# One-hots of the gates with two tokens innermost instead of four, and the steps of pair choice and gates dealt out over u's blocks

## The chip, the cores and the metric

The kernel runs on one NeuronCore of one Trainium2 chip. The metric is the device time of one execution in microseconds. The kernel before took 2054.61 us, the median of three runs (2054.53 to 3795.32). TensorE is called PE below, VectorE DVE, ScalarE ACT, GpSimd POOL and the queue that issues the DMAs SP.

## What is computed

Two transformer layers over 256 tokens of width 1024: an attention mixer with a projection in and out (in layer 0 a sparse one, in layer 1 one with a forget gate), and behind each mixer the expert network `peer_ffn`, which takes most of the time:

```python
def peer_ffn(x, w_q, sub_keys, u, v):
    q = (x @ w_q).reshape(B, S, PEER_HEADS, 2, hq)
    s_half = jnp.einsum('bshpc,hpkc->bshpk', q, sub_keys).astype(jnp.float32)
    top_s, top_i = lax.top_k(s_half, PEER_TOPK)                  # 16 of 128, twice per head
    cand_s = top_s[..., 0, :, None] + top_s[..., 1, None, :]
    cand_i = top_i[..., 0, :, None] * PEER_N_KEYS + top_i[..., 1, None, :]
    best_s, best_pos = lax.top_k(cand_s.reshape(B, S, PEER_HEADS, n_cand), PEER_TOPK)
    experts = jnp.take_along_axis(cand_i.reshape(B, S, PEER_HEADS, n_cand), best_pos, axis=-1)
    gate = jax.nn.softmax(best_s, axis=-1)
    ...
        h = jax.nn.gelu(jnp.einsum('ted,td->te', u[ec], xc))
        return jnp.einsum('te,ted->td', gc.astype(h.dtype) * h, v[ec])
```

Each token chooses 8 x 16 experts out of 16384 = 128 x 128. An expert's number is a pair of keys.

## The kernel before

The expert network is computed densely. In each layer `peer` walks over the 128 blocks of `u` (128 experts each). For one block, `load_split` (L679) fetches 512 KB, ACT rounds it to the matmul's short fp32 format (`hi`, L116) and DVE takes the rest (`lo`, L117); three buffers of each rotate. `feat_block` (L695) then makes 24 matmuls of 256 columns: `hi` by the tokens' high part (L699), `hi` by their low part (L702) and `lo` by their high part (L703). `values` (L921) applies gelu and multiplies by the gates of that block: where a token's gate is there already, DVE does it (L930); where it isn't, the gelu is stored (L926) and multiplied later. Behind u comes the same walk over the 128 blocks of `v` (L965 to L967), which gives the output. A stage ahead of u projects the queries (16 blocks of `wq`) and scores them against the keys on DVE (L733 to L737).

Between u's blocks the program issues other work in small steps, written as Python generators that yield after each step:

- `best_pairs` (L802 to L877), pair choice: for each half of the tokens (`tt`), DVE adds the candidates (L817), takes the best 16 per head (L824 to L828), turns positions into indices by masks and sums (L834, L837, L841, L847, L848, L852, L855, L859) and normalises the gates (L862 to L867). Then PE transposes the indices and gates (L872 to L874) and they are copied to `hkT`, with a token per column.
- `gate_steps` (L890 to L919), gates: for 8 tokens at a time DVE compares `hkT`'s rows with `iota` and gets one-hots `o2` and `oh` of fp16 (L898, L899), multiplies `oh` by the gate's low part into `ol` and by its high part in place (L901, L902); PE makes, per token, two matmuls with the one-hot `o2` as weights and `oh` or `ol` as the moving operand, 128 columns each (L908, L909): 16 matmuls, called a cluster below, of which there are 32 per layer. DVE multiplies the result into blocks that have their values already (L915); ACT stores it for the others (L917).

In the one-hots' tiles the order is group, key, token: with four tokens innermost, the 128 elements that one matmul reads lie four fp16 elements, 8 bytes, apart.

How many steps are issued behind each block is set at the end of `peer`: `now` counts a price per step (0.8 for any step of pair choice, 1.3 for any of the gates) and steps are taken while it is under 1.5 per block. Pair choice has 24 steps per half, 48 in all; the gates have 96. The order in which engines execute is not the issue order alone: a scheduler lists the instructions per engine by what it holds to be ready, and each engine then works strictly down its list. Instructions in `pin` keep program order.

At the very start (`nsa`, L302 to L350) PE gets matmuls whose result nobody reads: `keep_warm(8)`, 8 of 512 columns on bf16 zeros, then `keep_warm_r`, 30 on fp32 zeros (10 each of 256, 192 and 128 columns, L318), then the transposes of the first piece of x (`norm.piece`, L150), `keep_warm(3)`, and the first projection (L327, L328, L333).

Of the kernel before, what the change touches and what calls it, by code (L numbers as in the profile page):

```python
# [17 lines left out]
P = 128  # L18
# [21 lines left out]
def body(ctx, tc, A, out):  # L40
# [13 lines left out]
    maskb = const.tile([P, P], BF16, name="maskb")  # L54
    iota = const.tile([P, 2, P, 4], F16, name="iota")
    dram = ctx.enter_context(tc.tile_pool(name="dram", bufs=1, space=bass.MemoryType.DRAM))
# [51 lines left out]
    def late_consts():  # L108
        V.tensor_copy(identb, ident)
        GP.iota(iota, pattern=[[0, 2], [1, P], [0, 4]], base=0, channel_multiplier=0, allow_small_or_imprecise_dtypes=True)  # L110
        mtmp = t2k(P)
        SP.dma_start(mtmp, A["cmask"])
        V.tensor_copy(maskb, mtmp)
# [146 lines left out]
    def nsa():  # L260
# [50 lines left out]

        V.memset(HL[:, 12288:12288 + S].bitcast(F32), 0.0)
        wz = HL[:, 12288:12288 + S]

        def keep_warm_r(n, w):
            pt = pst("h")
            for _ in range(n):
                pin(PE.matmul(pt[:, :w], wz[:, :P], wz[:, :w], start=True, stop=True))  # L318

        o = [pst("m", bufs=4) for _ in range(2)]  # L320
# [15 lines left out]
        keep_warm(8)  # L336
        for w in (S, 192, P):
            keep_warm_r(10, w)
        norm.piece(0, 0, True)
# [366 lines left out]
    def peer(li, norm):  # L706
# [95 lines left out]
        def best_pairs():  # L802

            for tt in range(2):
# [4 lines left out]
                for a in range(9):  # L809
                    n = CAND_N[a] if a < 8 else 8  # L810
                    if a < 8:
                        i0 = top[:, tt, :, 1, 0:n]
                        i1 = top[:, tt, :, 0, a:a + 1].broadcast_to((P, 8, n))
                    else:
                        i0 = top[:, tt, :, 0, 8:16]
                        i1 = top[:, tt, :, 1, 0:1].broadcast_to((P, 8, n))
                    V.tensor_tensor(cand[:, tt, :, o_:o_ + n], i0, i1, ALU.add)  # L817
                    o_ += n
                    if a in (2, 8):
                        yield  # L820
                for hh in range(8):
                    c1 = cand[:, tt, hh]
                    c2 = cand2[:, hh % 2]
                    V.max(best[:, tt, hh, 0:8], c1)  # L824
                    V.max_index(pos[:, tt, hh, 0:8], best[:, tt, hh, 0:8], c1)
                    V.match_replace(c2, best[:, tt, hh, 0:8], c1, FMIN)
                    V.max(best[:, tt, hh, 8:16], c2)
                    V.max_index(pos[:, tt, hh, 8:16], best[:, tt, hh, 8:16], c2)  # L828
                    yield
                V.tensor_tensor(gf[:, tt], best[:, tt], best[:, tt, :, 0:1].broadcast_to((P, 8, 16)), ALU.subtract)  # L830

                V.tensor_copy(posh[:, tt], pos[:, tt])
                for hh in range(8):
                    V.tensor_tensor(msk[0][:, hh], posh[:, tt, hh].unsqueeze(1).broadcast_to((P, 16, 16)), st3, ALU.is_ge)  # L834
                    if hh % 4 == 3:
                        yield
                V.tensor_tensor(msk[0], msk[0], dl[:, tt].unsqueeze(3).broadcast_to((P, 8, 16, 16)), ALU.mult)  # L837
                yield
                for q in range(2):
                    hs = slice(4 * q, 4 * q + 4)  # L840
                    V.tensor_reduce(i12[:, tt, 0, hs], msk[0][:, hs].rearrange("p h j k -> p h k j"), AX.X, ALU.add)  # L841
                    yield

                V.tensor_scalar(bh[:, tt], posh[:, tt], -42.0, 0.0, ALU.add, ALU.max)
                V.tensor_tensor(bh[:, tt], posh[:, tt], bh[:, tt], ALU.subtract)
                for i, (st, ln) in enumerate(((16, 16), (24, 8), (29, 5), (33, 4), (36, 3), (38, 2), (40, 2), (42, 2))):
                    V.tensor_scalar(th[:, tt], posh[:, tt], float(st), float(ln), ALU.is_ge, ALU.mult)  # L847
                    V.tensor_tensor(bh[:, tt], bh[:, tt], th[:, tt], ALU.subtract)  # L848
                    if i % 4 == 3:
                        yield  # L850
                for hh in range(8):
                    V.tensor_tensor(msk[1][:, hh], bh[:, tt, hh].unsqueeze(1).broadcast_to((P, 16, 16)), jt3, ALU.is_equal)  # L852
                    if hh % 4 == 3:
                        yield
                V.tensor_tensor(msk[1], msk[1], idxh[:, tt, :, 1, :].unsqueeze(3).broadcast_to((P, 8, 16, 16)), ALU.mult)  # L855
                yield
                for q in range(2):
                    hs = slice(4 * q, 4 * q + 4)
                    V.tensor_reduce(i12[:, tt, 1, hs], msk[1][:, hs].rearrange("p h j k -> p h k j"), AX.X, ALU.add)  # L859
                    yield  # L860
                g3 = gf[:, tt]
# [5 lines left out]
                V.tensor_tensor(g3, g3, gs.unsqueeze(2).broadcast_to((P, 8, 16)), ALU.mult)  # L867
                yield

# [6 lines left out]
                V.tensor_tensor(hkT[:, 3, ts], pt[:, 2 * P:3 * P], hkT[:, 2, ts], ALU.subtract)  # L876
                yield  # L877

# [11 lines left out]
        def gate_steps():  # L890


            for t0 in range(0, S, 8):
                ohb, ol = t4k(2, 2, P, 4, dt=F16), t2k(2, P, 4, dt=F16)
                o2, oh = ohb[:, 0], ohb[:, 1]
                row = lambda i: (hkT[:, i, t0:t0 + 8].rearrange("p (q t) -> p q t", q=2)
                                 .unsqueeze(2).broadcast_to((P, 2, P, 4)))
                V.tensor_tensor(o2, iota, row(1), ALU.is_equal)  # L898
                V.tensor_tensor(oh, iota, row(0), ALU.is_equal)  # L899
                yield  # L900
# [10 lines left out]
                yield  # L911
                for q in range(2):
# [5 lines left out]
                    done[1] += 4  # L918
                yield  # L919

# [11 lines left out]

        aux = [(0.8, x) for x in (best_pairs,)] + [(1.3, gate_steps)]
        now, (cost, steps) = 0.0, (aux[0][0], aux[0][1]())
        aux.pop(0)
        for b in range(NB):
            values(b, feat_block(load_split(uT[b])))
            while steps is not None and now < 1.5 * (b + 1):
                if next(steps, 0) == 0:
                    cost, steps = (aux[0][0], aux[0][1]()) if aux else (0, None)  # L940
                    aux = aux[1:]
                now += cost
        for _ in steps or ():
            pass

# [156 lines left out]
```

## Time and profile before

| | us |
|---|---|
| median of three runs | 2054.61 |
| the profiled execution | 2047.41 |
| its span from first to last instruction | 2045.5 |
| u's walk, layer 0 (matmul starts to the last block's end) | 253.5 to 700.6 |
| u's walk, layer 1 | 1241.8 to 1689.0 |

The profile is of one execution. An engine's busy time counts matmuls that overlap in the pipeline with their whole length each, so a busy PE is judged here by how far apart its matmuls start and by how many there are in a stretch, not by its busy share. [...]

### The profile page before, as it was taken

Reading aid. Unit: us, or ns where it says so; the run is one execution under the profiler, and the core shown is the slowest. Engines: PE = TensorE matmul, PEld = TensorE weight load, DVE = VectorE, ACT = ScalarE, POOL = GpSimd, SP = SyncE. Lnnn points to the kernel's source line nnn. Section 1 sums busy time; section 2 is a strip of 40 time slices with the busy share of each in tenths; the row PEclk is TensorE's granted clock in tenths of the full one; section 3 lists DMA queues with packets and bytes.
Section 4 is the critical chain, followed back from the end, with each engine's and each line's share of the span. In section 5 each row is a group of like instructions: output and inputs, shape, how many; then the busy total and the mean of one; then the engine's idle time right before and its main releaser. Section 6 shows DMA issues by size and latency. Waiting matters only on the chain.

```text
span 2045.5 us, 34104 instructions
## 1 busy us (share of the span) xinstructions
PE 1995.8 (98%) x13121; PEld 1782.2 (87%) x13121; DVE 1422.5 (70%) x2973; ACT 1001.7 (49%) x1912; POOL 154.5 (8%) x98
## 2 busy tenths in 40 slices
PE   9999989999999999999999999999999999999998
PEld 6747989999999988888879799999999998888886
DVE  7576999677777555555576789976777755555555
ACT  5454644544444444444464654544444454444444
POOL 3010700000000000000050251000000000000001
PEclk9989999999999999999999999999999999999999
DMA  7701545444445676666664234544444456666664
GB/s 283 251 27 62 155 136 165 149 149 137 148 141 156 208 234 195 216 192 193 193 227 166 68 120 148 167 145 144 145 146 141 149 177 194 196 214 200 193 195 144
DMA packets 90193, 340.91 MB, mean 167 GB/s; under 512 B 9872, under 2 KB 12336, under 8 KB 84656
## 3 DMA queue, kind: packets, MB, share of 16 engines
q1 hardware_dynamic: 89744, 338.22, 52.6%
q8 instruction: 103, 1.69, 0.3%
q14 instruction: 58, 0.48, 0.1%
q10 hardware_dynamic: 288, 0.52, 0.1%
HBM read 334.48 MB, written 4.19 MB: 166 GB/s over the span
## 4 chain that ended last, share of the span: by engine, by line
PE 76%; DVE 16%; issue 4%; ACT 3%; DMA 1%; POOL 0%; SPq 0%; ACTq 0%; DVEq 0%
PE m L966 11%; PE m L965 11%; PE m L967 11%; PE h L703 8%; PE h L702 7%; PE h L699 7%; DVE lo L117 4%; PE m L908 3%; PE m L909 3%; ACT hi L116 3%; PE m L200 2%; PE m L201 2%; PE m L202 2%; DVE vhl L902 1%; DVE vraw L901 1%
## 5 line engine op out<-in xcount | busy, mean ns | idle before, releaser
L117 DVE TENSOR_TENSOR lo<-raw,hi 128x1024 fp32r<-128x1024 f32 x512 | 628.2, 1227 | 432.0 <-ACT hi L116 429.0
L116 ACT CAST hi<-raw 128x1024 fp32r<-128x1024 f32 (+1 forms) x576 | 577.4, 1005 | 671.6 <-PE m L967 293.4
L703 PE MATMUL h<-xh,lo 128*128 128x256 f32 x2048 | 583.9, 285 | 8.8 <-DVE lo L117 8.7
L702 PE MATMUL h<-xl,hi 128*128 128x256 f32 x2048 | 582.6, 284 | 0.0
L699 PE MATMUL h<-xh,hi 128*128 128x256 f32 x2048 | 581.7, 284 | 0.0
L703 PEld LDWEIGHTS h<-xh,lo 128*128 128x128 f32 x2048 | 390.4, 191 | 10.5 <-DVE lo L117 10.5
L966 PE MATMUL m<-lo,vhl 128*128 128x512 f32 x1024 | 398.9, 390 | 0.1
L965 PE MATMUL m<-hi,vhl 128*128 128x512 f32 x1024 | 399.0, 390 | 0.0
L967 PE MATMUL m<-hi,vhl 128*128 128x512 f32 x1024 | 398.8, 389 | 0.0
L699 PEld LDWEIGHTS h<-xh,hi 128*128 128x128 f32 x2048 | 390.0, 190 | 0.2
L702 PEld LDWEIGHTS h<-xl,hi 128*128 128x128 f32 x2048 | 390.0, 190 | 0.1
L967 PEld LDWEIGHTS m<-hi,vhl 128*128 128x128 f32 x1024 | 192.5, 188 | 40.1
L965 PEld LDWEIGHTS m<-hi,vhl 128*128 128x128 f32 x1024 | 192.5, 188 | 40.0
L966 PEld LDWEIGHTS m<-lo,vhl 128*128 128x128 f32 x1024 | 192.5, 188 | 40.0 <-DVE lo L117 0.5
L908 PE MATMUL m<-vhl 128*128 128x128 f16 x512 | 123.8, 295 | 3.7
L909 PE MATMUL m<-vraw,vhl 128*128 128x128 f16 x512 | 124.8, 297 | 0.0
L117 POOL TENSOR_TENSOR E<-arena,E 128x1024 fp32r<-128x1024 f32 (+1 forms) x20 | 47.0, 2364 | 956.3 <-ACT E L116 854.7
L117 POOL TENSOR_TENSOR lo<-raw,hi 128x512 fp32r<-128x512 f32 x64 | 90.3, 1426 | 101.5 <-ACT hi L116 101.1
L116 ACT CAST E<-arena 128x1024 fp32r<-128x1024 f32 (+2 forms) x68 | 63.1, 954 | 44.5 <-DMA arena<-in_w_in 26.5
L699 PE MATMUL h<-E,hi 128*128 128x256 f32 x240 | 71.0, 296 | 0.0
L917 ACT ACTIVATE arena<-m 128x256 f32<-128x256 f32 (+18 forms) x128 | 42.5, 338 | 57.4 <-DVE arena L915 43.2
L117 DVE TENSOR_TENSOR E<-arena,E 128x1024 fp32r<-128x1024 f32 (+2 forms) x48 | 56.6, 1196 | 19.3 <-ACT E L116 19.2
(286 smaller groups left out, 2553.6 us busy)
## 6 DMA issues: line engine op xcount, KB each, us to landing
raw<-in_u SPq DMA_DIRECT2D x256, 512.0 KB, 3.5
raw<-in_v SPq DMA_DIRECT2D x256, 512.0 KB, 3.6
arena<-in_w_in SPq DMA_DIRECT2D x18, 1024.0 KB, 4.9
raw<-in_wq SPq DMA_DIRECT2D x32, 512.0 KB, 3.7
arena<-in_w SPq DMA_DIRECT2D x8, 1024.0 KB, 5.4
arena<-in_w_out SPq DMA_DIRECT2D x8, 1024.0 KB, 5.1
hd<-arena SPq DMA_DIRECT2D x3, 1024.0 KB, 4.0
arena<-hd SPq DMA_DIRECT2D x3, 1024.0 KB, 5.3
```

Of the source, the lines that this page charges most:

```text
L116: ACT.copy(hi, raw)
L117: (eng or V).tensor_tensor(lo, raw, hi.bitcast(F32), ALU.subtract)
L200: PE.matmul(o[:, :n], sh[:, cc, tsl], wh[:, c], start=cc == 0, stop=False)
L699: t = PE.matmul(o[:, :S], hi[:, c % 4], sh[:, c], start=c == 0, stop=False)
L702: PE.matmul(o[:, :S], hi[:, c % 4], sl[:, c], start=False, stop=False)
L703: PE.matmul(o[:, :S], lo[:, c % 4], sh[:, c], start=False, stop=c == 7)
L908: PE.matmul(o, o2[:, q, :, i], oh[:, q, :, i], start=True, stop=False)
L909: PE.matmul(o, o2[:, q, :, i], ol[:, q, :, i], start=False, stop=True)
L917: ACT.activation(x, pgs[q][:, lo:hi], AF.Copy, scale=1.0 / GSC)
L965: PE.matmul(acc[tt][nh], gh[:, ts], vh, start=first, stop=False)
L966: PE.matmul(acc[tt][nh], gh[:, ts], vl, start=False, stop=False)
L967: PE.matmul(acc[tt][nh], gl[:, ts], vh, start=False, stop=last)
```

## The change

The group and token dimensions of the one-hots' tiles change from 2 x 4 to 4 x 2, with `iota` and the rows of `hkT` to match: still 8 tokens and 1024 elements per instruction, but a matmul's 128 elements lie two fp16 elements, 4 bytes, apart, for weights and moving operand alike, and DVE's innermost rows have two elements instead of four. Steps of pair choice and gates yield a price of their own, and the loop takes steps while the sum is under 1.62 per block. The prices add up to 34.8 for each half's pair choice (69.6 in all) and to 32 x 4.0 = 128 for the gates. The 30 fp32 matmuls at the start and the memset that they needed are dropped. All else is the same text; behind the dropped lines, lines have numbers lower by 8 to 10.

```diff
-    iota = const.tile([P, 2, P, 4], F16, name="iota")
+    iota = const.tile([P, 4, P, 2], F16, name="iota")
...
-        V.memset(HL[:, 12288:12288 + S].bitcast(F32), 0.0)
-        wz = HL[:, 12288:12288 + S]
-
-        def keep_warm_r(n, w):
-            pt = pst("h")
-            for _ in range(n):
-                pin(PE.matmul(pt[:, :w], wz[:, :P], wz[:, :w], start=True, stop=True))
...
         keep_warm(8)
-        for w in (S, 192, P):
-            keep_warm_r(10, w)
         norm.piece(0, 0, True)
...
                     V.max_index(pos[:, tt, hh, 8:16], best[:, tt, hh, 8:16], c2)
-                    yield
+                    yield 1.25
...
                 V.tensor_tensor(msk[0], msk[0], dl[:, tt].unsqueeze(3).broadcast_to((P, 8, 16, 16)), ALU.mult)
-                yield
+                yield 2.3
...
-                ohb, ol = t4k(2, 2, P, 4, dt=F16), t2k(2, P, 4, dt=F16)
+                ohb, ol = t4k(2, 4, P, 2, dt=F16), t2k(4, P, 2, dt=F16)
                 o2, oh = ohb[:, 0], ohb[:, 1]
-                row = lambda i: (hkT[:, i, t0:t0 + 8].rearrange("p (q t) -> p q t", q=2)
-                                 .unsqueeze(2).broadcast_to((P, 2, P, 4)))
+                row = lambda i: (hkT[:, i, t0:t0 + 8].rearrange("p (q t) -> p q t", q=4)
+                                 .unsqueeze(2).broadcast_to((P, 4, P, 2)))
                 V.tensor_tensor(o2, iota, row(1), ALU.is_equal)
                 V.tensor_tensor(oh, iota, row(0), ALU.is_equal)
-                yield
+                yield 1.4
...
-                        PE.matmul(o, o2[:, q, :, i], oh[:, q, :, i], start=True, stop=False)
-                        PE.matmul(o, o2[:, q, :, i], ol[:, q, :, i], start=False, stop=True)
+                        k, u = 2 * q + i // 2, i % 2
+                        PE.matmul(o, o2[:, k, :, u], oh[:, k, :, u], start=True, stop=False)
+                        PE.matmul(o, o2[:, k, :, u], ol[:, k, :, u], start=False, stop=True)
...
-        aux = [(0.8, x) for x in (best_pairs,)] + [(1.3, gate_steps)]
-        now, (cost, steps) = 0.0, (aux[0][0], aux[0][1]())
-        aux.pop(0)
+        def steps():
+            yield from best_pairs()
+            yield from gate_steps()
+
+        aux, spent = steps(), 0.0
         for b in range(NB):
             values(b, feat_block(load_split(uT[b])))
-            while steps is not None and now < 1.5 * (b + 1):
-                if next(steps, 0) == 0:
-                    cost, steps = (aux[0][0], aux[0][1]()) if aux else (0, None)
-                    aux = aux[1:]
-                now += cost
-        for _ in steps or ():
-            pass
+            while spent < 1.62 * (b + 1):
+                spent += next(aux, 1e9)
```

How the lists of the engines change is shown at two places. The first is DVE in u's walk of layer 0, in the first half's pair choice, where positions are turned into indices; `lo_...` is the low part of one u block, `arena` holds all of pair choice. Before:

```order
L834 TENSOR_TENSOR arena<-arena 128x256 x8
L117 TENSOR_TENSOR lo_2921<-raw_2918,hi_2920 128x1024
L837 TENSOR_TENSOR arena<-arena 128x2048
L117 TENSOR_TENSOR lo_2954<-raw_2951,hi_2953 128x1024
L841 TENSOR_REDUCE arena<-arena 128x64 x2
L844 TENSOR_SCALAR arena<-arena 128x128
L847 TENSOR_SCALAR arena<-arena 128x128
L117 TENSOR_TENSOR lo_3004<-raw_3001,hi_3003 128x1024
```

And now (L824 is the former L834, L827 the former L837, L831 the former L841):

```order
L824 TENSOR_TENSOR arena<-arena 128x256 x5
L117 TENSOR_TENSOR lo_2913<-raw_2910,hi_2912 128x1024
L824 TENSOR_TENSOR arena<-arena 128x256 x3
L834 TENSOR_SCALAR arena<-arena 128x128
L837 TENSOR_SCALAR arena<-arena 128x128
L827 TENSOR_TENSOR arena<-arena 128x2048
L117 TENSOR_TENSOR lo_2949<-raw_2946,hi_2948 128x1024
L831 TENSOR_REDUCE arena<-arena 128x64
L117 TENSOR_TENSOR lo_2982<-raw_2979,hi_2981 128x1024
L831 TENSOR_REDUCE arena<-arena 128x64
L117 TENSOR_TENSOR lo_3015<-raw_3012,hi_3014 128x1024
```

The two long sums now have a low part of u between them. Over the whole of pair choice, though, its last two long sums stand between the 28th and the 29th low part of the layer in both lists. What moved away from there are the gates' first one-hots: eight of those instructions stand ahead of the 28th low part before, and one now. Behind pair choice, the 14 gaps from that behind the 32nd low part to that behind the 45th, of which all but one hold work of the gates before, are empty now. On PE, the transposes of the first half come behind 22 blocks of u instead of 14, those of the second behind 43 instead of 28; the first cluster of gates comes behind 44 blocks instead of 28 and the last behind 122 instead of 109.

The second place is ACT at the start of the program; `E_...` takes the parts of the first weights, `xh` the high part of the first tokens, `g_...` the transposes of x. Before:

```order
L120 ACTIVATE arena,ss_86<-arena 128x512
L116 CAST E_85<-arena 128x512 x4
L120 ACTIVATE arena,ss_87<-arena 128x512
L120 ACTIVATE arena,ss_86<-arena 128x512
L116 CAST E_85<-arena 128x512 x2
L156 ACTIVATE xh<-g_134,cst 128x128 x4
```

And now:

```order
L120 ACTIVATE arena,ss_86<-arena 128x512
L156 ACTIVATE xh<-g_100,cst 128x128 x4
L116 CAST E_85<-arena 128x512 x4
L120 ACTIVATE arena,ss_87<-arena 128x512
L120 ACTIVATE arena,ss_86<-arena 128x512
```

The high part of the first tokens now stands ahead of the rounding of the weights instead of behind six of its eight instructions.

## Rows read from the trace of the kernel before

**Rows 1.** The page's head and its list of busy engines.

```profile
span 2045.5 us, 34104 instructions
PE 1995.8 (98%) x13121; PEld 1782.2 (87%) x13121; DVE 1422.5 (70%) x2973; ACT 1001.7 (49%) x1912; POOL 154.5 (8%) x98
```

**Rows 2.** Stretches of u's walk, layer 0, for L699 alone (8 per block).

```profile
core 0: us, PE busy (x) PEld busy (x), PEclk, DMA share, GB/s
253.40:339.40 86.00, 59.04 (x202) 40.26 (x203) 0.94 0.50 154
339.40:650.20 310.80, 191.93 (x681) 128.29 (x681) 1.00 0.48 146
650.20:701.00 50.80, 39.84 (x142) 26.54 (x141) 1.00 0.58 177
```

**Rows 3.** The same stretches, all engines.

```profile
core 0: us, PE busy (x) PEld busy (x) DVE busy (x) ACT busy (x) POOL busy (x), PEclk, DMA share, GB/s
253.40:339.40 86.00, 78.74 (x616) 77.44 (x616) 84.82 (x308) 39.56 (x60) 0.00 (x0) 0.94 0.50 154
339.40:650.20 310.80, 307.31 (x2558) 303.66 (x2557) 231.10 (x400) 145.10 (x346) 0.00 (x0) 1.00 0.48 146
650.20:701.00 50.80, 50.80 (x429) 50.76 (x428) 29.82 (x39) 25.13 (x41) 0.00 (x0) 1.00 0.58 177
```

**Rows 4.** Timeline of PE around one cluster of gates (start us, length us).

```profile
381.59 0.28 PE L703 MATMUL h<-xh,lo 128*128 128x256 f32 x1
381.71 0.28 PE L699 MATMUL h<-xh,hi 128*128 128x256 f32 x1
382.05 0.28 PE L908 MATMUL m<-vhl 128*128 128x128 f16 x1
382.15 0.30 PE L909 MATMUL m<-vraw,vhl 128*128 128x128 f16 x1
...
383.81 0.29 PE L909 MATMUL m<-vraw,vhl 128*128 128x128 f16 x1
383.86 0.37 PE L702 MATMUL h<-xl,hi 128*128 128x256 f32 x1
384.06 0.28 PE L703 MATMUL h<-xh,lo 128*128 128x256 f32 x1
```

**Rows 5.** PE's warm-up matmuls: 9 of L318 at 128 columns, 3 of L310 (start, length).

```profile
7.40 1.17 PE L318 MATMUL h<-E 128*128 128x128 f32 x9
8.86 0.81 PE L310 MATMUL h<-arena 128*128 128x512 bf16 x3
```

**Rows 6.** Groups by line and shape (count, busy us, mean ns, idle before).

```profile
L117 DVE TENSOR_TENSOR lo<-raw,hi 128x1024 fp32r<-128x1024 f32 x512 | 628.2, 1227 | 432.0 <-ACT hi L116 429.0
L898 DVE TENSOR_TENSOR vhl<-iota,hkT 128x1024 f16<-128x1024 f16 x64 | 43.6, 682 | 2.1 <-PE m L909 2.1
L837 DVE TENSOR_TENSOR arena<-arena 128x2048 f16<-128x2048 f16 x4 | 9.1, 2280 | 0.0
L834 DVE TENSOR_TENSOR arena<-arena 128x256 f16<-128x256 f16 x32 | 6.8, 279 | 0.0
```

**Rows 7.** Timeline of the start (start us, length us, idle before and releaser).

```profile
4.21 4.36 PE L318 MATMUL h<-E 128*128 128x256 f32 x30
4.35 0.63 ACT L120 ACTIVATE arena<-arena 128x512 f32<-128x512 f32 x1 [2.35 <-DMA arena<-in_x]
8.40 0.62 PE L150 MATMUL g<-cst,arena 128*128 128x128 f32 x4
11.30 1.14 ACT L116 CAST E<-arena 128x512 fp32r<-128x512 f32 x2 [0.55 <-DMA arena<-in_w_in]
12.34 1.13 ACT L156 ACTIVATE xh<-g,cst 128x128 fp32r<-128x128 f32 x4
12.75 0.80 PE L327 MATMUL m<-E,xh 128*128 128x512 f32 x1 [3.08 <-ACT xh L156]
```

**Rows 8.** A stretch at the start, all engines, columns as in rows 3.

```profile
12.00:16.00 4.00, 3.25 (x10) 2.56 (x11) 3.63 (x12) 3.12 (x9) 3.15 (x2) 0.57 1.06 429
```

More of the change, by code (lines that the diff above doesn't have):

```diff
@@ L109, in late_consts @@
         V.tensor_copy(identb, ident)
-        GP.iota(iota, pattern=[[0, 2], [1, P], [0, 4]], base=0, channel_multiplier=0, allow_small_or_imprecise_dtypes=True)
+        GP.iota(iota, pattern=[[0, 4], [1, P], [0, 2]], base=0, channel_multiplier=0, allow_small_or_imprecise_dtypes=True)
         mtmp = t2k(P)
@@ L819, in best_pairs @@
                     if a in (2, 8):
-                        yield
+                        yield 1.0
                 for hh in range(8):
@@ L835, in best_pairs @@
                     if hh % 4 == 3:
-                        yield
+                        yield 1.3
                 V.tensor_tensor(msk[0], msk[0], dl[:, tt].unsqueeze(3).broadcast_to((P, 8, 16, 16)), ALU.mult)
-                yield
+                yield 2.3
                 for q in range(2):
@@ L841, in best_pairs @@
                     V.tensor_reduce(i12[:, tt, 0, hs], msk[0][:, hs].rearrange("p h j k -> p h k j"), AX.X, ALU.add)
-                    yield
+                    yield 2.1
                 V.tensor_scalar(bh[:, tt], posh[:, tt], -42.0, 0.0, ALU.add, ALU.max)
@@ L849, in best_pairs @@
                     if i % 4 == 3:
-                        yield
+                        yield 1.7
                 for hh in range(8):
@@ L853, in best_pairs @@
                     if hh % 4 == 3:
-                        yield
+                        yield 1.15
                 V.tensor_tensor(msk[1], msk[1], idxh[:, tt, :, 1, :].unsqueeze(3).broadcast_to((P, 8, 16, 16)), ALU.mult)
-                yield
+                yield 2.3
                 for q in range(2):
@@ L859, in best_pairs @@
                     V.tensor_reduce(i12[:, tt, 1, hs], msk[1][:, hs].rearrange("p h j k -> p h k j"), AX.X, ALU.add)
-                    yield
+                    yield 2.1
                 g3 = gf[:, tt]
@@ L867, in best_pairs @@
                 V.tensor_tensor(g3, g3, gs.unsqueeze(2).broadcast_to((P, 8, 16)), ALU.mult)
-                yield
+                yield 1.2
                 pt = pst("g")
@@ L876, in best_pairs @@
                 V.tensor_tensor(hkT[:, 3, ts], pt[:, 2 * P:3 * P], hkT[:, 2, ts], ALU.subtract)
-                yield
+                yield 0.3
         done = [0, 0]
@@ L893, in gate_steps @@
             for t0 in range(0, S, 8):
-                ohb, ol = t4k(2, 2, P, 4, dt=F16), t2k(2, P, 4, dt=F16)
+                ohb, ol = t4k(2, 4, P, 2, dt=F16), t2k(4, P, 2, dt=F16)
                 o2, oh = ohb[:, 0], ohb[:, 1]
-                row = lambda i: (hkT[:, i, t0:t0 + 8].rearrange("p (q t) -> p q t", q=2)
-                                 .unsqueeze(2).broadcast_to((P, 2, P, 4)))
+                row = lambda i: (hkT[:, i, t0:t0 + 8].rearrange("p (q t) -> p q t", q=4)
+                                 .unsqueeze(2).broadcast_to((P, 4, P, 2)))
                 V.tensor_tensor(o2, iota, row(1), ALU.is_equal)
                 V.tensor_tensor(oh, iota, row(0), ALU.is_equal)
-                yield
+                yield 1.4
                 V.tensor_tensor(ol, oh, row(3), ALU.mult)
@@ L907, in gate_steps @@
                         o = pg[:, i * P:(i + 1) * P]
-                        PE.matmul(o, o2[:, q, :, i], oh[:, q, :, i], start=True, stop=False)
-                        PE.matmul(o, o2[:, q, :, i], ol[:, q, :, i], start=False, stop=True)
+                        k, u = 2 * q + i // 2, i % 2
+                        PE.matmul(o, o2[:, k, :, u], oh[:, k, :, u], start=True, stop=False)
+                        PE.matmul(o, o2[:, k, :, u], ol[:, k, :, u], start=False, stop=True)
                     pgs.append(pg.rearrange("p (t i) -> p i t", t=4))
-                yield
+                yield 1.4
                 for q in range(2):
@@ L918, in gate_steps @@
                     done[1] += 4
-                yield
+                yield 1.2
         def values(b, o):
```

## Prediction

> **What bounds the kernel now.** I read the page's head first. The span is 2045.5 us and PE counts as busy for 98% of it [rows 1]. That share says little, since a matmul's length overlaps the next one's start, so I went on to how many matmuls start in a stretch. The view of stretches for L699, which occurs 8 times per block of u, gives that [rows 2]. In the last stretch, behind all the gates, there are 142, which is 17.75 blocks in 50.8 us: 2.86 us per block, with nothing else on PE and the matmuls 0.12 us apart [rows 2, 4]. This is PE's own pace. In the first stretch, pair choice, there are 202: 25.25 blocks, worth 72.2 us at that pace, take 86.0, so 13.8 us are lost. In the same stretch DVE is busy for 84.82 of 86 us [rows 3]: there DVE is the bound and PE waits for low parts. In the middle stretch, the gates, 681 make 85.1 blocks, worth 243.5 us; the other 67.3 of its 310.8 us go to 32 clusters of gate matmuls, 2.10 us each. DVE has 231.1 us of work there, 74% [rows 3], so here PE is the bound and each nanosecond of a gate matmul counts in the span.
>
> The timeline around a cluster shows where the 2.10 us go [rows 4]. From L908 at 382.05 to the last L909 at 383.81 lie 15 steps, so 0.117 us each; the other 0.34 us are the change from u's matmuls to the gates' and back. Strange is the 0.117: these matmuls have 128 columns, and those of u with 256 columns follow each other in the same time.
>
> **The gate matmuls.** Nothing in the list changes but the distance of the elements: 8 bytes before, 4 bytes now. Matmul count stays 512 per layer. u's matmuls read 256 columns of fp32 side by side, 4 bytes apart, in 0.12 us; the gates' read 128 columns 8 bytes apart in 0.117. Both pass over 1024 bytes per partition. I take it that PE's reading sets the pace by the bytes that it passes over. [...] From below, the warm-up matmuls on bf16 side by side bound it: three of 512 columns take 0.81 us in all with the last one's drain [rows 5]; their starts are some 0.215 apart, 0.054 per 128 columns. From above stands no change, 0.117; near it lies the row of 128 columns of fp32, where 9 take 1.17 us, 8 steps and the last one's 0.27, so 0.11 each [rows 5]: 128 columns can cost that even at 4 bytes. I choose 0.065, as that row's weights are fp32, of twice the bytes. A cluster then takes 15 x 0.065 + 0.34 = 1.32 us and saves 0.78; 64 clusters in two layers save 50 us. At 0.054 it is 60, at 0.11 it is 7.
>
> [...]
>
> Can the gain be used? What covers the clusters now is DVE, which must keep up with a shorter PE. Before, DVE has 231.1 / 32 = 7.22 us of work per cluster. Now a cluster comes every 2.5 blocks, so PE needs 2.5 x 2.86 + 1.32 = 8.47 us and DVE, with 0.16 block less, some 7.0: 83%. L915 gets wider, since more blocks have their values when gates arrive; from 67 blocks on the mean to 83 this is 8 x 16 elements, some 0.13 us. It fits.
>
> **The one-hots on DVE.** Four instructions per cluster, 0.682 us each for 1024 elements [rows 6]. Two rows say what sets that: L834 takes 0.279 for 256 elements, with 16 in an innermost row; L837, whose innermost element repeats, takes 2.28 for 2048. So the first kind costs 0.53 ns per element, two at a time, and the second 1.05, one at a time; both have 0.14 us fixed. Rows of four go two at a time; a row of two is still one pair. I count no change; one at a time it would be 1.22 us each, 2.16 more per cluster.
>
> **Dealing out the steps.** The prices allow 1.62 us of work per block, beside a low part of 1.23 us [rows 6]: that is what 2.86 us hold. But the scheduler doesn't follow them. By its list the whole of pair choice still stands ahead of the 29th low part, as before, and the gaps behind are empty. So over these blocks DVE still has more than PE and PE still waits. What leaves the stretch are seven one-hots, 7 x 0.68 = 4.8 us of DVE; and the long sums have low parts between them, so the three buffers cover more, and the transposes of the second half, behind 43 blocks instead of 28, no longer meet a DVE that is late. I count 7 us per layer, 14 in all, with 0 and 13.8 per layer as bounds: nothing gained, and the whole loss of the stretch. What is late next in that stretch is DVE again, with its low parts.
>
> Later gates cost nothing at the end: the last cluster stands behind block 122 of 128, and six blocks (17 us) lie between it and v.
>
> **The start.** The 30 matmuls on zeros run from 4.21 to 8.57 us, and the transposes of x, whose first piece is there at 4.35, come behind them at 8.40 [rows 7]. But the first projection starts at 12.75, behind ACT's L156 at 12.34, which stands on ACT behind weights that arrive at 11.30. In the new list L156 comes ahead of the weights, so with 0.62 us of transposes and 1.13 of L156 the projection may begin some 6 us earlier. It then waits for the same weights at 11.30, and the granted clock, 0.57 on the mean from 12 to 16 us [rows 8], may sink earlier and for longer. I count 3 us gained, between 6 gained and 3 lost; the attention behind it has other waits that may eat it.
>
> **The sum.** The profiled execution took 2047.4 us, 7.2 below the median of the runs. From 2047.4 go 50, 14 and 3: 1980.4. With the same distance the median to be expected is 1987.6; I say 1988.
>
> **Rivals.**
>
> First, the distance is not what limits the gate matmuls. [...] As a mechanism of this kernel: the weight load of each matmul, one per 128 columns, takes the time, and 0.11 or 0.117 stays [rows 5]. For it speaks that row; against it, that 1024 bytes cost the same 0.12 in u and in the gates. Then only dealing out and the start are left: 2054.6 - 17 = 2038. Chance 0.12.
>
> Second, rows of two are not packed on DVE. At 1.22 us per one-hot, DVE has 7.0 + 2.16 = 9.2 us per cluster against PE's 8.47 and becomes the bound: 64 x 0.7 = 45 us of the 67 go, which makes 2033. Against it: a row of four is packed at its full rate. Chance 0.07.
>
> Third, slower: short rows cost DVE more than packing ever gave, at L898 to L902. The 67 us gained are 1.05 per cluster, so DVE may take 8.47 + 1.05 - 7.0 = 2.5 us more per cluster before the kernel is slower, 0.63 per one-hot: from 1.31 us each it decides. If a row of two took three ticks of the 1.05 ns instead of one, a one-hot would take 0.14 + 512 x 3.15 ns = 1.75 us, DVE 11.3 us per cluster, 2.8 over PE: 64 x 2.8 = 180 on 1988, 2168. Nothing in the trace has such rows. Chance 0.03.
>
> Fourth, the dealing out does what its prices say and the whole loss of pair choice goes: 14 more, 1974. Against it stands the list. Chance 0.04.
>
> **How the numbers follow.** My forecast has 0.74. Its own range goes from 0.054 us per gate matmul with half of the dealing out's upside (some 1972) to a pace midway between 0.065 and 0.11, 0.0875 us, with the start gaining nothing (15 x 0.0295 x 64 = 28 and 14 gained, 2012). The range for 8 in 10 reaches from 1968, where the fourth case has its faster end, to 2038, which takes in the first and second rivals; the third stays out. About 2% of 2054.6, 41 us, can be told from no change: faster means under 2013.5. The forecast with nearly all its range and the fourth case lie there, 0.76; the first two rivals and the forecast's slow end are within 2%, 0.20; the third and something unforeseen at the start are slower, 0.04.
>
> **What would show it.** Right: the gate matmuls start 0.065 us apart and a cluster costs 1.3 us; the one-hots stay at 0.68 us; in the stretch of pair choice DVE is still full, and PE loses 5 to 9 us there; DVE is busy for some 83% among the gates; L156 and L327 begin before 8 us. Wrong: matmuls still 0.11 or more apart, one-hots of 1.2 us, PE waiting for low parts or for L901 and L902 among the gates, or the attention ahead of u longer than its 253 us.

## The result, and the profile after

The changed kernel took 1980.81 us, the median of four runs (1977.24 to 1986.79), against 2054.57 of the kernel before on the same chip: a ratio of 0.9653, with a 95% interval of 0.961 to 0.9696. The ratio leaves out one slow run of the kernel before, which took 3795.32 us. The forecast was 1988. The profiled execution took 1977.24 us. Its head, which answers to [rows 1]:

```profile
span 1975.5 us, 34015 instructions
PE 1929.8 (98%) x13091; PEld 1716.9 (87%) x13091; DVE 1421.9 (72%) x2964; ACT 991.4 (50%) x1882; POOL 158.7 (8%) x98
```

PE has 30 matmuls less, the warm-ups, and is still "98% busy" in a span that is 70 us shorter; that share told nothing before and tells nothing now. Lines are 9 or 10 lower than before (u's matmuls are L689, L692 and L693, the gates' L899 and L900, the one-hots L888 to L892). The stretches of u's walk in layer 0 for L689 alone answer to [rows 2] (PEclk is PE's granted clock as a share of full speed); the first ends with the 43rd block, just ahead of the first cluster of gates at 383.50, the second behind the last cluster:

```profile
core 0: us, PE busy (x) PEld busy (x), PEclk, DMA share, GB/s
243.40:380.50 137.10, 98.25 (x344) 65.67 (x344) 0.98 0.55 166
380.50:646.40 265.90, 181.17 (x640) 120.86 (x641) 1.00 0.52 159
646.40:660.70 14.30, 11.28 (x41) 7.51 (x40) 1.00 0.56 185
```

The stretch ahead of the gates now has 344 / 8 = 43 blocks. At PE's own pace, 2.856 us each (24 matmuls 0.119 apart), they are worth 122.8, so 14.3 of the 137.1 us are lost, where 13.8 were lost before. The gates' stretch has 80 blocks, worth 228.5; the other 37.4 us are 32 clusters of 1.17 us, where they were 2.10. So by this cut the whole gain of the walk lies in the gates' stretch, 29.9 us, and none in pair choice. The same walk for all engines, with pair choice cut in three, answers to [rows 3]:

```profile
core 0: us, PE busy (x) PEld busy (x) DVE busy (x) ACT busy (x) POOL busy (x), PEclk, DMA share, GB/s
243.40:313.70 70.30, 66.94 (x537) 64.39 (x536) 70.20 (x270) 32.89 (x50) 0.00 (x0) 1.00 0.52 158
313.70:323.50 9.80, 5.41 (x29) 4.92 (x28) 9.16 (x30) 3.51 (x6) 0.00 (x0) 0.65 0.52 153
323.50:380.50 57.00, 57.00 (x483) 57.00 (x482) 35.74 (x34) 26.63 (x40) 0.00 (x0) 1.00 0.58 178
380.50:646.40 265.90, 264.37 (x2436) 261.07 (x2435) 218.12 (x393) 133.58 (x319) 0.00 (x0) 1.00 0.52 159
```

This view shows why dealing out the steps brought nothing in pair choice. Over the first 22 blocks DVE is busy for 70.20 of 70.30 us and PE loses 7.5 (22 blocks are worth 62.8); block 22 alone takes 9.8 us, 6.9 too many; and over the 20 blocks behind it DVE has 35.74 us of work in 57.00 and PE runs at its own pace, losing nothing. The work is still bunched at the front, and DVE idles 37% of the stretch in which it could have been done. Among the gates DVE is busy for 218.12 of 265.90 us, 82%.

The timeline of PE around one cluster (start us, length us), answering to [rows 4]:

```profile
397.16 0.28 PE L689 MATMUL h<-xh,hi 128*128 128x256 f32 x1
397.50 0.22 PE L899 MATMUL m<-vhl 128*128 128x128 f16 x1
397.55 0.22 PE L900 MATMUL m<-vraw,vhl 128*128 128x128 f16 x1
...
398.36 0.22 PE L900 MATMUL m<-vraw,vhl 128*128 128x128 f16 x1
398.38 0.36 PE L692 MATMUL h<-xl,hi 128*128 128x256 f32 x1
398.59 0.28 PE L693 MATMUL h<-xh,lo 128*128 128x256 f32 x1
```

From the first gate matmul to the last lie 15 steps and 0.86 us: 0.057 each, half of the 0.117 before. What the cluster takes from u is 1.43 us from L689 to L693 less the two steps of 0.12 that would be there anyway, 1.19.

DVE's groups by line and shape (count, busy us, mean ns, idle before) answer to [rows 6]:

```profile
L117 DVE TENSOR_TENSOR lo<-raw,hi 128x1024 fp32r<-128x1024 f32 x512 | 628.3, 1227 | 401.3 <-ACT hi L116 397.9
L888 DVE TENSOR_TENSOR vhl<-iota,hkT 128x1024 f16<-128x1024 f16 x64 | 43.6, 681 | 0.0
```

A one-hot costs 681 ns as before (682): rows of two elements cost DVE nothing here. What happens at block 22 stands in the timeline there (start, length, idle before and its releaser in brackets):

```profile
310.73 4.12 DVE L831 TENSOR_REDUCE arena<-arena 128x64 f32<-128x1024 f16 x2
...
313.92 0.27 PE L692 MATMUL h<-xl,hi 128*128 128x256 f32 x1
...
314.74 1.25 DVE L117 TENSOR_TENSOR lo<-raw,hi 128x1024 fp32r<-128x1024 f32 x1
316.04 0.39 PE L693 MATMUL h<-xh,lo 128*128 128x256 f32 x1 [1.85 <-DVE lo L117]
...
319.33 0.28 DVE L857 TENSOR_TENSOR arena<-arena,gs 128x128 f32<-128x128 f32 x1
319.67 0.48 PE L863 MATMUL g<-cst,arena 128*128 128x128 f32 x1 [2.54 <-DVE arena L857]
...
320.16 0.41 PE L693 MATMUL h<-xh,lo 128*128 128x256 f32 x1
...
323.14 0.37 PE L692 MATMUL h<-xl,hi 128*128 128x256 f32 x1
```

PE waits first for a low part that stood behind two sums on DVE (L831, 4.12 us), and then for 2.54 us at L863, the transpose of the first half's gates, which stands in PE's list ahead of the rest of that block, whose low part is ready: DVE gets to the gates' last step, L857, only at 319.33. The two waits are 4.4 of the 6.9 us. Part of the rest is the granted clock: read in pieces of half a us it is 1.00 up to 316.50, 0.50 from there to 323.00, 0.68 in the next piece and 1.00 again from 323.50, so some 6.8 of the 9.8 us with the mean of 0.65 are at the lower level. From 320.16 to 323.14 u's matmuls start 0.213 us apart instead of 0.119, which over these 14 steps is 1.3 us.

The start, answering to [rows 7]:

```profile
4.56 1.06 PE L150 MATMUL g<-cst,arena 128*128 128x128 f32 x4
5.66 1.14 ACT L156 ACTIVATE xh<-g,cst 128x128 fp32r<-128x128 f32 x4 [0.64 <-PE g L150]
6.68 2.19 ACT L116 CAST E<-arena 128x512 fp32r<-128x512 f32 x4
7.36 0.49 PE L319 MATMUL m<-E,xh 128*128 128x512 f32 x1 [0.90 <-ACT E L116]
10.74 1.14 ACT L116 CAST E<-arena 128x512 fp32r<-128x512 f32 x2 [0.52 <-DMA arena<-in_w_in]
```

The first projection begins at 7.36 us (L327 began at 12.75 before). Its weights are there: the wait for a DMA that I read in [rows 7] at 11.30 returns at 10.74, and is that of a later part of the weights.

Over the whole program the profiled spans differ by 2045.5 - 1975.5 = 70.0 us: u's walk of layer 0 starts 10.0 us earlier (243.45 against 253.47), takes 29.9 less (417.29 against 447.17), the work between the walks takes 0.8 less, u's walk of layer 1 29.4 less (417.77 against 447.18), and the rest is equal to 0.1.

### The profile page after: what moved, and what is told of

Read it like the earlier page. It is cut to its first block, busy times and chain, and to the rows that moved or that the text cites. A ratio compares the mean times of both kernels' runs of the same rounds, so it can differ in the third digit from the quotient of the medians.

```text
span 1975.5 us, 34015 instructions
## 1 busy us (share of the span) xinstructions
PE 1929.8 (98%) x13091; PEld 1716.9 (87%) x13091; DVE 1421.9 (72%) x2964; ACT 991.4 (50%) x1882; POOL 158.7 (8%) x98
## 4 chain that ended last, share of the span: by engine, by line
PE 77%; DVE 15%; ACT 3%; issue 3%; DMA 1%; POOL 0%; SPq 0%; ACTq 0%; DVEq 0%; POOLq 0%
PE m L953 12%; PE m L955 12%; PE m L954 12%; PE h L692 8%; PE h L693 8%; PE h L689 8%; DVE lo L117 4%; ACT hi L116 2%; PE m L201 2%; PE m L899 2%; PE m L200 2%; PE m L202 2%; PE m L900 1%; DVE vhl L892 1%; DVE vraw L891 1%
## 5 line engine op out<-in xcount | busy, mean ns | idle before, releaser
L693 PE MATMUL h<-xh,lo 128*128 128x256 f32 x2048 | 584.5, 285 | 10.1 <-DVE lo L117 9.6
L692 PE MATMUL h<-xl,hi 128*128 128x256 f32 x2048 | 581.9, 284 | 0.0
L689 PE MATMUL h<-xh,hi 128*128 128x256 f32 x2048 | 581.5, 284 | 0.3 <-ACT E L917 0.2
L693 PEld LDWEIGHTS h<-xh,lo 128*128 128x128 f32 x2048 | 388.1, 190 | 14.7 <-DVE lo L117 14.5
L689 PEld LDWEIGHTS h<-xh,hi 128*128 128x128 f32 x2048 | 388.3, 190 | 0.9 <-ACT E L917 0.8
L692 PEld LDWEIGHTS h<-xl,hi 128*128 128x128 f32 x2048 | 388.4, 190 | 0.0
L908 ACT ACTIVATE arena<-m 128x256 f32<-128x256 f32 (+24 forms) x128 | 38.6, 312 | 72.5 <-DVE arena L906 71.2
L689 PE MATMUL h<-E,hi 128*128 128x256 f32 x240 | 71.0, 296 | 0.0
L693 PE MATMUL h<-E,lo 128*128 128x256 f32 x240 | 68.8, 287 | 0.0
L692 PE MATMUL h<-E,hi 128*128 128x256 f32 x240 | 68.6, 286 | 0.0
```

The source lines that it names most:

```text
L689: t = PE.matmul(o[:, :S], hi[:, c % 4], sh[:, c], start=c == 0, stop=False)
L692: PE.matmul(o[:, :S], hi[:, c % 4], sl[:, c], start=False, stop=False)
L693: PE.matmul(o[:, :S], lo[:, c % 4], sh[:, c], start=False, stop=c == 7)
```

## The experiments

All kernels below compute the whole result. Walk lengths are from the first L689 matmul to the end of the last block, layer 0 and layer 1.

**The layout alone (e1) and the steps alone (e2).** e1 is the kernel before with only this changed:

```diff
-    iota = const.tile([P, 2, P, 4], F16, name="iota")
+    iota = const.tile([P, 4, P, 2], F16, name="iota")
...
-                        PE.matmul(o, o2[:, q, :, i], oh[:, q, :, i], start=True, stop=False)
+                        PE.matmul(o, o2[:, k, :, u], oh[:, k, :, u], start=True, stop=False)
```

> The kernel before with the two-token layout alone. Theory (PE's reading distance is the gain, and DVE's old dealing doesn't stand in its way): gate matmuls 0.057 us apart, 64 clusters each 0.92 us shorter, 2054.6 - 59 = 1996, within 1988 to 2004. Rival (the shorter clusters can only be used with the new dealing of the steps): DVE becomes the bound among the gates, less than 40 us gained, above 2015.

e2 is the kernel before with the prices and the new loop alone:

```diff
-                        yield
+                        yield 1.0
...
-            while steps is not None and now < 1.5 * (b + 1):
+            while spent < 1.62 * (b + 1):
```

> The kernel before with the new dealing of the steps alone. Theory (the scheduler's list keeps pair choice in the first 30 blocks, so the dealing moves the loss instead of removing it): 2 to 3 us per layer gained, 2049, within 2042 to 2055. Rival (the dealing takes the loss of pair choice away, as forecast or more): 14 to 28 us gained, 2027 to 2041.

e1 took 1991.88 us, a ratio of 0.9686 (0.9627 to 0.9745); its gate matmuls start 0.057 us apart and its walks take 419.31 and 419.06 us, together 56.0 less than before's. e2 took 2044.4, a ratio of 0.9969 (0.9936 to 1.0001); its walks take 445.21 and 446.32, together 2.8 less. So the layout carries the gain; e2's interval holds 1, so what the prices do is read from the walks. What they add to the layout is the difference of e1's walks and those of the changed kernel, 2.0 and 1.3 us.

The place of this gain is the second half's transposes. Ahead of the block with the first cluster the changed kernel loses more than e1, 14.3 and 15.0 us against 12.5 and 12.6. But where the gates begin, PE waits for DVE at L872 in the kernel before, and in the changed kernel it hardly does. The kernel before, then the changed one:

```profile
348.26 0.33 PE L872 MATMUL g<-cst,arena 128*128 128x128 f32 x1 [1.65 <-DVE arena L859]
```

```profile
384.61 0.33 PE L863 MATMUL g<-cst,arena 128*128 128x128 f32 x1 [0.24 <-DVE arena L857]
```

In e1 this wait is 2.64 us in layer 0 and 2.06 in layer 1, and its gates' stretch costs 1.29 us per cluster where that of the changed kernel costs 1.17.

**The start alone (e3).** The kernel before without the 30 matmuls:

```diff
-        for w in (S, 192, P):
-            keep_warm_r(10, w)
```

> The kernel before without the 30 warm-up matmuls alone. Theory (the start's gain is theirs): the first projection starts 5 us earlier, u's walk of layer 0 some 10 us earlier, 2045, within 2041 to 2050. Rival (the gain at the start came from another order that the whole program happened to get): u's walk starts within 5 us of before, above 2050.

It took 2039.57 us, a ratio of 0.9952 (0.993 to 0.9974). Its first projection begins at 7.01 us, but u's walk at 249.37, only 4.1 earlier than in before's profile, as the rival said, while the time is below what either gave. Neither fits as a whole, and e9 to e11 below say why. By the medians the three parts alone gain 58.4, 5.9 and 10.7 us, 74.9 together, and the whole change 73.8: the parts add up.

**The moving operand or the weights (e5, e6).** Of this pair and of e7 to e11 there is one run each, so they are read by what their traces show. Both are the changed kernel; in e5 the weights `o2` lie 8 bytes apart and the moving operand 4, in e6 the other way round (e6's difference to e5):

```diff
-                o2, oh, ol = lay(ohb[:, 0], 2), lay(ohb[:, 1], 4), lay(ol, 4)
+                o2, oh, ol = lay(ohb[:, 0], 4), lay(ohb[:, 1], 2), lay(ol, 2)
...
```

> The changed kernel with the weights' one-hot o2 back at 8 bytes between elements and the moving one-hots oh and ol left at 4. Theory (the moving operand's distance sets the gate matmuls' pace): 0.057 us apart as in the changed kernel, u's walk of a layer 417 us, time near 1981. Rival (the weight load's distance sets it): 0.117 apart, 64 clusters 0.9 us longer, u's walk 446 us, near 2040.

> The reverse: weights at 4 bytes, moving one-hots back at 8. Theory (the moving operand sets the pace): 0.117 us apart, u's walk 446 us, near 2040. Rival (the weight load sets it): 0.057 apart, 417 us, near 1981.

e5 took 1987.32 us and e6 2041.59 (before beside them 2049.73). A cluster in the timeline of e5:

```profile
455.74 0.22 PE L901 MATMUL m<-vhl 128*128 128x128 f16 x1
455.80 0.22 PE L902 MATMUL m<-vraw,vhl 128*128 128x128 f16 x1
...
456.63 0.22 PE L902 MATMUL m<-vraw,vhl 128*128 128x128 f16 x1
```

And of e6, from its third matmul on:

```profile
...
451.93 0.30 PE L901 MATMUL m<-vhl 128*128 128x128 f16 x1
452.05 0.30 PE L902 MATMUL m<-vraw,vhl 128*128 128x128 f16 x1
...
453.44 0.29 PE L902 MATMUL m<-vraw,vhl 128*128 128x128 f16 x1
```

In e5 15 steps take 0.89 us, 0.059 each; in e6 13 steps take 1.51, 0.116 each. So in these runs it is the moving operand's distance that sets the pace. The weight loads tell less. First e5's group, then that of the changed kernel, then e6's:

```profile
L902 PEld LDWEIGHTS <-vhl 128*128 128x128 f16 x512 | 58.3, 114 | 5.1 <-issue 1.4
```

```profile
L900 PEld LDWEIGHTS <-vhl 128*128 128x128 f16 x512 | 49.5, 97 | 6.0 <-issue 1.4
```

```profile
L902 PEld LDWEIGHTS <-vhl 128*128 128x128 f16 x512 | 58.1, 114 | 7.1 <-issue 2.9
```

With the weights at 8 bytes a load takes 114 ns instead of 97, nearly two matmul steps, and yet the matmuls follow each other in 59: these loads overlap, and the weights' distance costs 2 ns a matmul (59 against the changed kernel's 57). But e6's loads take 114 too, with weights at 4 bytes and a slow moving operand, so the length of a load by itself does not tell how far apart its weights lie.

**Keys innermost (e7).** The changed kernel with a matmul's 128 elements side by side, 2 bytes apart. DVE's innermost row is then 128 long, with `hkT`'s element repeated in it:

```diff
-                ohb, ol = t4k(2, 4, P, 2, dt=F16), t2k(4, P, 2, dt=F16)
+                ohb, ol = t4k(2, 8, P, dt=F16), t2k(8, P, dt=F16)
...
```

> The changed kernel with the keys innermost, so elements lie 2 bytes apart on PE, and on DVE the row of hkT repeats one element along the innermost dimension. Theory (DVE takes such a row one element at a time, and 4 bytes were near enough for PE): one-hots 1.22 us each, gate matmuls still 0.055 to 0.057 apart, DVE becomes the bound among the gates, u's walk some 442 us, near 2035. Rival (DVE's price doesn't hang on the innermost row): 0.68 us, 417 us, near 1981.

It took 2028.5 us. The gate matmuls start 0.056 us apart, no better than at 4 bytes, but each one-hot costs DVE 1.216 us, and DVE is now the fuller engine among the gates, here in e7's groups by form and in its stretch of the gates:

```profile
L887 DVE TENSOR_TENSOR vhl<-iota,hkT 128x1024 f16<-128x1024 f16 x64 | 77.9, 1216 | 0.0
```

```profile
397.00:690.00 293.00, 276.40 (x2497) 268.87 (x2496) 281.63 (x402) 138.70 (x330) 0.00 (x0) 0.99 0.49 149
```

DVE is busy for 281.63 of 293.00 us, 96%, and PE idles 16.6. The walks take 437.88 and 434.92. So of the three distances that were run, two tokens innermost is the one at which neither engine pays: with the keys innermost DVE does (1.216 us a one-hot against 0.681), with four tokens PE does (0.117 us a matmul against 0.057).

**Late transposes (e8).** The changed kernel with the transposes of both halves behind the whole of pair choice, so that none of them stands in PE's list while DVE is behind:

```diff
+            for tt in range(2):
                 pt = pst("g")
                 PE.transpose(pt[:, 0:P], i12[:, tt, 0].rearrange("p h k -> p (h k)"), ident)
```

> The changed kernel with the transposes of both halves issued at the end of pair choice, so that PE meets none at block 22. Theory (at block 22 PE waits for a DVE that is late with everything, the low parts too): the gap there shrinks from 9.8 us to 5 or 6, since the low part behind it comes no earlier, u's walk some 412 to 414 us. Rival (the transposes alone make the gap): it goes down to under 4 us, u's walk 410 us or less.

It took 1972.56 us; the walks take 415.60 and 414.81 and block 22 takes 6.74 and 5.20 us instead of 9.75 and 9.89. So L863's place in PE's list cost 3.0 and 4.7 us there, and the lower clock is part of that: the changed kernel has 6.8 us at a PEclk of 0.50 at this block in both layers, while e8 has 3.4 us of it in layer 0 (u's matmuls start 0.214 us apart from 318.62 to 321.83), and its block in layer 1 is another 1.54 us shorter. The walks gain less, 1.7 and 3.0 us, as some blocks behind it take up to 3.84 us, and stay above the 412 to 414 of the theory. Most of the remainder is the low part, as e8's timeline shows at the same block:

```profile
316.55 1.27 DVE L117 TENSOR_TENSOR lo<-raw,hi 128x1024 fp32r<-128x1024 f32 x1
317.87 0.39 PE L693 MATMUL h<-xh,lo 128*128 128x256 f32 x1 [2.12 <-DVE lo L117]
```

**The steps dealt out in the lists, too (e4).** In the changed kernel prices decide only the order of issue; the scheduler takes a step of pair choice as soon as its inputs are there, and that is at once. e4 lets the steps of a block be listed only behind the low part of that block:

```diff
-        (eng or V).tensor_tensor(lo, raw, hi.bitcast(F32), ALU.subtract)
+        lo_mark[0] = (eng or V).tensor_tensor(lo, raw, hi.bitcast(F32), ALU.subtract).ins
...
-            while spent < 1.62 * (b + 1):
-                spent += next(aux, 1e9)
+            with tc.issue_after(lo_mark[0]):
+                while spent < 1.62 * (b + 1):
+                    spent += next(aux, 1e9)
```

> The changed kernel, with each block's steps tied behind the low part of that block on DVE, so that the list follows the prices. Theory (DVE is late in pair choice because its list packs the steps, and PE's transposes of the first half wait for that): the 16 us lost per layer in pair choice shrink to 4 to 8, 8 to 12 gained per layer, 1980.8 - 20 = 1961, within 1954 to 1968. Rival (the wait at the transposes is due to their place on PE, not to DVE's being late): the gap of 9.8 us at block 22 stays, above 1972.

It took 1959.44 us, a ratio of 0.9526 (0.9468 to 0.9584), and is faster than both kernels. Its walks take 405.81 and 405.99 us; 3.2 us are lost ahead of the block with the first cluster in each layer, where the changed kernel loses 14.3 and 15.0, and no block among the first 43 takes over 3.97. The two halves of its pair choice, 22 blocks and the rest, in the view of all engines:

```profile
256.60:321.80 65.20, 64.25 (x536) 63.62 (x536) 62.02 (x207) 33.09 (x51) 0.00 (x0) 1.00 0.58 178
321.80:382.60 60.80, 60.39 (x509) 60.19 (x508) 54.58 (x126) 29.75 (x46) 0.00 (x0) 1.00 0.56 182
```

DVE has 62.02 us of work in 65.20 and then 54.58 in 60.80: 95% and 90%, where the changed kernel had all of the first and 63% of the last stretch. The granted clock stays at 1.00. The same work, spread, costs PE 11 to 12 us less per layer.

**The same programs again (e9, e10, e11).** u's walk started anywhere between 243 and 261 us in these runs, in kernels that differ ahead of u by little but the warm-ups. So I ran the changed kernel, the one before and e4 once more, without an edit.

> The changed kernel once more, unaltered, with a new profile. Theory: in the attention ahead of u TensorE's granted clock falls at other places and for other lengths in each execution of the same program, and the start of u's walk in layer 0 moves with it, by some 0.4 us per us at the lower level. u then starts at 240.6 + 0.41 times the us at the lower level up to there (243.45 was with 6.8 us of it in the attention), anywhere from 243 to 257. Rival: the lists set the start of u; it lies within 1 us of 243.5 again. Both: u's walk takes 417 to 418 us with one gap of 9 to 10 us at block 22.

> The kernel before once more, unaltered, with a new profile. Theory: u's walk in layer 0 starts at 248 + 0.41 times the us at the lower clock from 90 us on, which need not be the 13.6 us of the first profile: anywhere from 250 to 262. Rival: within 1 us of 253.5 again. Both: u's walk takes 447 to 448 us.

> The dealt version of e4 once more, unaltered. Theory: its late start of u (256.68) came from 37.6 us at the lower clock and not from its lists; with fewer us of it u starts earlier, by 0.41 us for each. Rival: the lists of this version delay u; it starts within 1 us of 256.7 whatever the clock does. Both: u's walk takes 405 to 407 us.

They took 1978.29, 2067.96 and 1957.5 us (before beside them 2047.54). The stretch from 90 to 176 us, the attention of layer 0, for all engines with the granted clock behind POOL; the kernel before in its first profile:

```profile
90.00:176.00 86.00, 80.88 (x437) 42.74 (x437) 63.69 (x187) 52.64 (x177) 14.01 (x6) 0.92 0.18 65
```

The kernel before again (e10):

```profile
90.00:176.00 86.00, 84.13 (x347) 42.81 (x336) 45.13 (x141) 40.21 (x132) 9.31 (x4) 0.60 0.17 57
```

e4:

```profile
90.00:176.00 86.00, 80.86 (x361) 41.08 (x361) 58.87 (x176) 47.41 (x164) 14.05 (x6) 0.78 0.12 43
```

e4 again (e11):

```profile
90.00:176.00 86.00, 80.66 (x419) 43.99 (x419) 64.33 (x184) 50.06 (x168) 14.04 (x6) 0.92 0.16 57
```

The same program gets through 437 matmuls in these 86 us at a mean clock of 0.92 and through 347 at 0.60. With 1.00 and 0.50 as the levels (in e10 the mean is 1.00 from 90 to 100 us and 0.50 from 110 to 170), a mean of 0.92 is 86 x 0.08 / 0.5 = 13.8 us at the lower one, and 0.60 is 68.8. u's walk starts at 253.47 and 276.91: 23.4 us later for 55.0 more at the lower level, 0.43 for each. In e4 and e11 it is 256.68 and 246.36 at 0.78 and 0.92, 10.3 for 24.1: 0.43 again. The changed kernel, by chance, had 0.96 both times and started u at 243.45 and 244.06, so that e9 alone fits its rival as well. The theory held in e10 and e11, though e10 went beyond the 262 that it gave as the end. The walks were what they had been (417.59, 447.74 and 405.93 in layer 0). What makes the clock fall in one execution and not in another is open: no run shows it.

With 0.43 us taken off for each us at the lower level, u's walk starts at 247.5 and 247.3 in the two profiles of before, and at 240.5 in the changed kernel (243.45 - 0.43 x 6.9) and 240.4 in e4 and e11. Dropping the warm-ups is thus worth some 7.0 us at u's start, and e3 fits: 249.37 with 0.88, that is 20.6 us, comes to 240.5. Worked out in the same way, e1 and e2 come to 248.0 and 247.4, e9 to 241.1, e6, e7 and e8 to between 239.3 and 242.4; e5 doesn't fit, at 244.4. With this scatter the 7.0 are an estimate, good to 2 or 3 us.

## Why the prediction was right

**The sum.** The forecast for the profiled execution was 1980.4, and it took 1977.24. The terms, however, were less good than their sum: gates 50, dealing out 14 and start 3 were forecast; 56.0 (e1's walks against before's), 3.3 (e1's walks less those after) and 10.0 came, with 0.7 elsewhere. The sum came out so near by luck: errors of 6 and 7 one way cancelled one of 11 the other way.

**The gate matmuls: right in kind, 6 us too small.** The moving operand's distance was the limit, in e1 (0.117 us at 8 bytes, 0.057 at 4) and, more sharply, in e5 and e6 (0.059 with it at 4 bytes, 0.116 at 8). That the bytes passed over set the pace in general was my guess and isn't shown: half of them again, at 2 bytes, still took 0.056 (e7), and 128 columns of fp32 at 4 bytes took 0.11 [rows 5]. The mis-sized term is the pace, 0.065 forecast and 0.057 measured. No run shows the 0.065, which was my estimate; at 4 bytes the runs showed 0.057 (the changed kernel and e1) and 0.059 (e5). The row of bf16 matmuls side by side, 0.054 per 128 columns [rows 5], was the nearer one; I had left it for an fp32 row with other weights, and in e5 the weights' distance made only 2 ns. The rest of a cluster, 0.34 us, was as forecast: 1.17 to 1.19 in all, less 0.86, leaves 0.31 to 0.33.

**The one-hots: right.** 0.681 us were forecast unchanged, and the price that I gave for elements taken one at a time, 1.22, is what e7 measured, 1.216. With 82% against the 83% forecast, DVE covers the shorter clusters.

**Dealing out: wrong, 11 us too much.** The step that failed is that the long sums with low parts between them and the later transposes would halve the loss of pair choice, to "5 to 9" us. I had read from the order that pair choice still stands ahead of the 29th low part, and that was the right reading: the loss stayed, 14.3 us against 13.8. I had looked at the second half's transposes, which move behind 43 blocks and do meet a DVE that is done (a wait of 0.24 us, where e1 has 2.64 and 2.06; there lie the 3.3 us), and not at the first half's, behind 22 blocks: by my own numbers DVE is fullest just there. At block 22 PE waits for a low part and for L863, the clock falls (0.65 on the mean), and 6.9 us are lost. e8 takes 3.0 and 4.7 us off this block by moving those transposes alone. That the prices themselves were sound shows in e4, which makes the lists follow them.

**The start: too small, and partly luck.** L156 and the first projection moved as forecast, but I took the wait at 11.30 [rows 7] for the first weights, and it is a later part's. So the projection gained 5.4 us and not 3, and by the estimate above some 7.0 arrive at u; where the 1.6 between come from isn't shown, and they are within the scatter. The other 2.9 of the 10.0 are 6.9 us less at the lower clock in the attention (0.96 against 0.92), which differ between executions of one program. The fear that without warm-ups the clock would stay low for longer at the start did not come true: in the first 90 us the mean is 0.98 in both,

```profile
0.00:90.00 90.00, 84.02 (x598) 64.44 (x599) 56.60 (x133) 41.04 (x76) 19.57 (x17) 0.98 0.76 268
```

before, and after

```profile
0.00:90.00 90.00, 85.85 (x622) 64.66 (x623) 62.93 (x142) 46.02 (x90) 23.74 (x17) 0.98 0.81 289
```

with 622 matmuls started instead of 598, of which 30 were the warm-ups.

**The rivals.** The first, that the distance is not the limit, fell: 8 bytes cost 0.117 and 4 cost 0.057 with nothing else changed in e1. Its mechanism, that the weight load takes the time, fell with it: pairs of a load and a matmul of 128 columns follow each other in 57 ns in the changed kernel. The second rival, rows of two unpacked, fell in the changed kernel, and e7, where another layout does make a one-hot cost 1.216 us, came out at 2028.5 where the rival had 2033. The third, slower, needed one-hots of over 1.31 us; even those of e7, 1.216 us, stay under that. The fourth, that the whole loss of pair choice goes, did not happen, but with the lists made to follow (e4, e11) it nearly does, and its price was right in size: of the 13.8 us per layer that it wanted gone, 3.2 stay.

## What to carry to other kernels

Look at how far apart a moving operand's elements lie: 128 columns of fp16 took 0.117 us at 8 bytes in these runs, 0.057 at 4 and 0.056 at 2. Look at the innermost row of the producing vector instruction as well: with a pair that is really in memory it took 0.681 us here, with one element repeated 1.216. The layout between both extremes can serve both engines, as it did here. A price list that sets the order of issue did little here (3.3 us in two layers), since this scheduler sorts by readiness: read the list of the engine that waits, and tie the steps to what they must not overtake. Cut a "full" stretch into pieces before spreading work over it, since one part may be full (DVE busy for 70.20 of 70.30 us here) and the next a third empty (35.74 of 57.00).

## What the runs showed of the hardware

PE's pace for 128 fp16 columns was 0.117 us at 8 bytes, 0.057 at 4 and 0.056 at 2, so below 4 bytes 0.001 us was left to gain. The weights' distance cost 2 ns a matmul in e5: at 8 bytes their loads took 114 ns instead of 97, and they overlapped so far that matmuls followed at 59 ns instead of 57.

DVE took rows of two fp16 elements at 0.681 us per 1024 elements and rows of four at 0.682, although the middle dimension of one operand repeats; where the innermost dimension repeats (e7), it took 1.216.

The clock is the widest spread that I had not expected: in one and the same program 13.8 us of the attention ran at the lower level, 0.50, in one execution and 68.8 in another, with u's start at 253 and 277. What PE did where it fell, in the changed kernel (all engines, columns as above):

```profile
100.00:110.00 10.00, 6.40 (x32) 4.49 (x33) 7.93 (x28) 4.02 (x17) 0.00 (x0) 0.66 0.00 0
...
90.00:176.00 86.00, 80.68 (x430) 45.02 (x430) 64.63 (x183) 50.35 (x169) 14.03 (x6) 0.96 0.16 56
```

It was busy for 6.40 of 10 us there, and for 80.68 of 86 over the stage. In u's walk of layer 0 the changed kernel's clock fell at block 22, where PE waited 1.85 and 2.54 us; in e4, without such waits, it was 1.00 there. A profile's start of a later stage should be compared with another's only at an equal clock ahead of it.
